# DeltaNet's last chunk of 16 tokens: four heads stacked on the partitions

## The chip, the cores and the metric

One core of a Trainium2 chip runs the whole program in one launch. The metric is the device time of that launch in microseconds, lower is better. TensorE (PE) does the matmuls, VectorE (DVE) and ScalarE (ACT) the elementwise work, GpSimd (POOL) some masks, and SyncE (SP) issues the DMAs. TensorE's clock has two levels, 1.2 and 2.4 GHz; the profile shows it as a granted clock of 0.50 and 1.00.

## The reference

A decoder trunk on 256 tokens and 16 meta tokens ahead of them (272 in all, model width 2048): one gated DeltaNet layer with its MLP, then one differential-attention layer with its MLP, everything in float32. The DeltaNet layer has 32 value heads of width 128; two value heads share a query and key head. Per head it is, cut to what matters:

```python
proj = h @ w_in                                   # q, k, v, gate, b, a
qkv = silu(causal_depthwise_conv(qkv, conv_w))
q, k = l2_normalize(q) * 128 ** -0.5, l2_normalize(k)
beta = sigmoid(b_logit); g = -exp(a_log) * softplus(a_logit + dt_bias)
# by chunks, with the state S (128 x 128):
G = cumsum(g); decay = exp(G_i - G_j) below the diagonal
a_kk = strictly_lower((k * beta) @ k.T * decay)
u, w = solve(I + a_kk, [v * beta, k * beta * exp(G)])
v_new = u - w @ S
o = (q * exp(G)) @ S + ((q @ k.T) * decay) @ v_new
S = S * exp(G_last) + (k * exp(G_last - G)).T @ v_new
o = rms_norm(o, o_norm) * silu(z);  out = o @ w_out
```

## The kernel before

`trunk` keeps the activations on chip with features on the partitions and tokens in the free dimension, 128x272 tiles. Each float32 weight product is three matmuls (`mm3`, L146): the weight and the activation are each split into a high and a low part, and hi x hi (L152), lo x hi (L155) and hi x lo (L156) are added in PSUM. A weight tile of 1 MB is loaded by SP (L120, into `wraw`, three buffers), then halved: ACT makes `whi` of 128x1024 (L137), DVE `wlo` (L139), in a ring of three. One half serves 8 steps of 3 matmuls. These matmuls, 272 columns each, are called the big products below.

The DeltaNet layer (`gdn`, L503) works on 8 groups of 4 value heads. For each group the big products of `w_in` run (`ps_in`, later `ps_out` for `w_out`), and between them the small work of the delta rule. The tokens are cut into chunks of 128, 128 and 16 (`CH`), numbered 0, 1 and 2; chunk 2 of 16 tokens is the one that the change is about. Per group and chunk:

- `keys` and `stats` (L636): transposes of q and k by chunk (`ps_kn`, L649), and sums of squares on ACT (`sqk`, L654).
- `products` (L666): the norms, a broadcast load of the group's cumulated log decays (`gb`, L686), masks on POOL (L688, L690), k by k and k by q (`ps_u`, L706), decays on ACT (`dec`, L710), and their product on DVE (`UA`, L712). The 16x16 diagonal blocks go to DRAM (L718, L721).
- `solve` (L737): inverts the 16x16 blocks of the group's heads, and loads the inverses (`DT`, L755; `DT3` for chunk 2, L757).
- `values` (L759): transposes of v (`ps_v`, L771) and scaled copies (`nv`, L773).
- `core` (L796): the recurrence. Per chunk, `ps_ks` (L880) and `R` (L884), for the long chunks the merging of the block inverses (`ps_e`, L840, is its first matmul), then `ps_w` (L916), `w` (L924), the state (`ps_s`, L929), `ps_o` (L941), `ov` (L947), squares (L951), the norm (L959 to L963, with `rsqrt` at L105 to L111), the scale (L966), and in `turned` the transposes back (`ps_ot`, L810) and their eviction into `oT` (L812). `oT` is split into `oh` and `ol` (L979, L980), on which the big products of `w_out` wait.

In chunk 2 every one of these is done per head, on 16 partitions: four `ps_w` of 16x16 weights, four `ps_o`, four `R`, and so on; `ps_ks` puts k and q of a key head side by side in `KQ3` (48 columns of weights).

The order of the work is written by `Flow` (L57): generators with due times stand in a heap, and each step of `mm3` moves its clock by `flow.tick(3 * N / 2400.0)`; what is due is emitted there. A scheduler then sets the order of each engine's queue. Group 7, the last, uses the shorter steps of `STEP7`, and its chunk 2 stands directly ahead of the last big products of `w_out`. In `decays` (L542), once at the head, the log decays of all heads are cumulated and stored to DRAM (`g_dram`, L584), from which every group's `gb` is read. SP also issues the loads of small constants between the first weight loads.

Of the kernel before, what the change touches and what calls it, by code (L numbers as in the profile page):

```python
# [31 lines left out]
GB = 4  # L32
HOLD = 1
# [469 lines left out]
def gdn(ctx, tc, a, e):  # L503
# [21 lines left out]
    gt = ctx.enter_context(tc.tile_pool(name="gt", bufs=2))  # L525
    gk = ctx.enter_context(tc.tile_pool(name="gk", bufs=4))
# [15 lines left out]
    def decays(ps):  # L542
# [29 lines left out]
        nc.vector.reciprocal(bt, bt)  # L572
        yield GATES[1]
# [10 lines left out]
        nc.sync.dma_start(g_dram, rows)  # L584
        G, GL = gnat[:, 0], gnat[:, 1]
# [5 lines left out]
        nc.scalar.activation(eLast, eLast, AF.Exp)  # L591
        gated.append(True)

    g_dram = dram.tile([32, L], F32, name="g_dram", bufs=1)
# [9 lines left out]
    DT3 = gc.tile([NM, HB, NM], F32, name="DT3")  # L604
    KQ3 = gc.tile([P, 2, 64], F32, name="KQ3")
# [30 lines left out]
    def keys(b):  # L636

        g = {"done": False, "free": False, "laid": False, "gates": 0, "values": 0, "chunk": 0,
             "prev": gs[-1] if gs else None}
        st = gt.tile([P, 2, 3, 2], F32, tag="st", name="st")  # L640
        nc.vector.memset(st, 1.0)
        kq = g["kq"] = gk.tile([P, 2, 2, L], F32, tag="kq", name="kq", bufs=2)
        kn = g["kn"] = gk.tile([P, 2, 2, P], F32, tag="kn", name="kn", bufs=2)

        def stats(h, t):
            yield SLACKST
            pk = psk.tile([P, 512], F32, tag="k", name="ps_kn")
            for c, (o, n) in enumerate(CH):
                nc.tensor.transpose(pk[:n, c * P:(c + 1) * P], kq[:, h, t, o:o + n], ident)  # L649
            if t == 0:  # L650
                nc.scalar.copy(kn[:, :, h, :], pk[:, :256].rearrange("p (c d) -> p c d", d=P))
            for c, (o, n) in enumerate(CH):
                sq = gt.tile([P, P], F32, tag="dec", name="sqk", bufs=2)
                nc.scalar.activation(sq[:n], pk[:n, c * P:(c + 1) * P], AF.Square, accum_out=st[:n, t, c, h:h + 1])  # L654
            if (h, t) == (1, 0):
                yield from products(b, g, st)

        for h in range(2):
            for t, m in ((1, 2 * b + h), (0, 16 + 2 * b + h)):
                ps = proj(m)  # L660
                conv_silu(ps, m, kq[:, h, t, :])
                flow.add(stats(h, t))
        return g

    def products(b, g, st):
        kq, prev = g["kq"], g["prev"]  # L666
# [15 lines left out]
        nc.vector.tensor_tensor(sup, sup, heads(eLast, b), ALU.mult)
        nc.vector.tensor_scalar(rq, rs[:, 1, :, :, None].broadcast_to([P, 3, 2, 2]), P ** -0.5, None, ALU.mult)
# [6 lines left out]
        nc.gpsimd.affine_select(gb[:NM, :, 256:L], gb[:NM, :, 256:L], pattern=[[0, HB], [1, NM]], base=0,  # L690
                                channel_multiplier=-1, compare_op=ALU.is_ge, fill=NEG)
# [3 lines left out]
        for c, (o, n) in enumerate(CH):  # L695
            while prev and prev["chunk"] < min(c, 1):
                yield 1.0
            if c < 2:
                ua = gk.tile([P, HB, 2, P], F32, tag="UA", name="UA", bufs=3)
            else:  # L700
                ua = gk.tile([NM, HB, 2, NM], F32, tag="UA3", name="UA3", bufs=2)
            UA.append(ua)
            for h in range(2):
# [3 lines left out]
                for r in range(2):  # L707
# [4 lines left out]
                    nc.vector.scalar_tensor_tensor(ua[:, hv], pu_v, negc[:n, c, h, r:r + 1],  # L712
                                                   dec[:n, None, :n].broadcast_to([n, 2, n]), ALU.mult, ALU.mult)
                yield UGAP
            if c < 2:
                for bl in range(8):
                    q = slice(NM * bl, NM * bl + NM)
                    nc.sync.dma_start(scr[c, :, bl].rearrange("h j i -> j h i"), ua[q, :, 0, q])  # L718
                below(ua, NM)
            else:  # L720
                nc.sync.dma_start(scr3.rearrange("h j i -> j h i"), ua[:, :, 0, :])  # L721
# [15 lines left out]
    def solve(scr, scr3):  # L737
# [19 lines left out]
        nc.sync.dma_start(DT3, scr4.rearrange("h m j -> m h j"))  # L757

    def values(b, g):  # L759
# [3 lines left out]
        def turned(hv, vt):  # L763
# [3 lines left out]
            if not nv:  # L767
                nv.extend(gk.tile([P, HB, P], F32, tag="nv", name="nv", bufs=4) for _ in CH)
            pv = psk.tile([P, 512], F32, tag="k", name="ps_v")
            for c, (o, n) in enumerate(CH):  # L770
                nc.tensor.transpose(pv[:n, c * P:(c + 1) * P], vt[:, o:o + n], ident)  # L771
            for c, (o, n) in enumerate(CH):
                nc.scalar.activation(nv[c][:n, hv], pv[:n, c * P:(c + 1) * P], AF.Copy,  # L773
                                     scale=g["nk"][:n, c, hv // 2:hv // 2 + 1])
            g["values"] += 1

        for hv in range(HB):
# [4 lines left out]
            conv_silu(ps, m, vt)  # L782
            flow.add(turned(hv, vt))
# [11 lines left out]
    def core(b, g):  # L795
# [7 lines left out]
        def turned(c, o, n, ov):  # L803
# [5 lines left out]
            for hv in range(HB):  # L809
                nc.tensor.transpose(pT[:, hv * n:(hv + 1) * n], ov[:n, hv], ident[:n, :n])  # L810
# [9 lines left out]
        ms = gt.tile([P, len(CH), HB], F32, tag="o_ms", name="o_ms")  # L820
# [42 lines left out]
        for c, (o, n) in enumerate(CH):  # L863
            if c == 0:
                R = nv[0]
            else:
                left = lambda h, t: kq[:, h, t, o:o + n]
                pS, pSv = bank("ps_ks")
                if c < 2:
                    pQ, pQv = bank("ps_qs")  # L870
                    banks = ((pS[:n], 0), (pQ[:n], 1))
                else:
# [3 lines left out]
                    banks = ((pS[:32 + n], 0),)  # L876
                    pQv = pSv[32:]
                for ps, t in banks:
                    for h in range(2):
                        nc.tensor.matmul(ps[:, 256 * h:256 * h + 256], left(h, t), S[:, 2 * h:2 * h + 2, :],  # L880
                                         start=True, stop=True)
                R = work("R")
                for hv in range(HB):
                    nc.vector.scalar_tensor_tensor(R[:n, hv], pSv[:n, hv], neG[:n, c, HB * b + hv:HB * b + hv + 1],  # L884
                                                   nv[c][:n, hv], ALU.mult, ALU.add)
                ov = work("ov")
                nc.scalar.copy(ov[:n], pQv[:n])
# [23 lines left out]
            else:  # L911
                z, dt = R, DT3
            yield step
            _, pw = bank("ps_w")
            for hv in range(HB):
                nc.tensor.matmul(pw[:n, hv], dt[:, hv, :], z[:n, hv], start=True, stop=True)  # L916
            if c == 2:
                g["free"] = True
            if c < 2:
# [3 lines left out]
            w = work("w")  # L923
            nc.scalar.copy(w[:n], pw[:n])  # L924
            yield step
            if c < 2:
# [12 lines left out]
            _, po = bank("ps_o")  # L939
            for hv in range(HB):  # L940
                nc.tensor.matmul(po[:n, hv], UA[c][:, hv, 1, :], w[:n, hv], start=True, stop=True)  # L941
            if c == 0:
                ov = work("ov")
                nc.scalar.activation(ov, po, AF.Copy, scale=-1.0)
            else:
                for hv in range(HB):
                    nc.vector.scalar_tensor_tensor(ov[:n, hv], ov[:n, hv], eG[:n, c, HB * b + hv:HB * b + hv + 1],  # L947
                                                   po[:n, hv], ALU.mult, ALU.subtract)

            for hv in range(HB):  # L950
                nc.scalar.activation(po[:n, hv], ov[:n, hv], AF.Square, accum_out=ms[:n, c, hv:hv + 1])  # L951
            outs.append((c, o, n, ov))
            if b == NB - 1 or c == len(CH) - 1:
                c0 = outs[0][0]
                k = HB * len(outs)
                pn = n if len(outs) == 1 else P
                mc = ms[:pn, c0:c + 1].rearrange("p c h -> p (c h)")
                rqc = rq[:pn, c0:c + 1].rearrange("p c h r -> p (c h r)")
# [3 lines left out]
                ri = rsqrt(mc, "rso%d" % k, [P, k], pn)  # L962
                nc.vector.tensor_tensor(ri, ri, rqc, ALU.mult)  # L963
                for i, (cc, oo, nn, ot) in enumerate(outs):
                    for hv in range(HB):
                        nc.scalar.activation(ot[:nn, hv], ot[:nn, hv], AF.Copy, scale=ri[:nn, HB * i + hv:HB * i + hv + 1])  # L966
# [311 lines left out]
```

## Time and profile before

| | |
|---|---|
| three runs | 3022.2, 3023.15, 3023.69 us (median 3023.15) |
| profiled execution | 3024.88 us, span 3023.1 us, mean granted clock 0.993 |
| TensorE busy | 2981.0 us, 99% of the span, 23747 matmuls |
| DVE, ACT, POOL busy | 1943.6 us (64%), 1490.1 us (49%), 205.2 us (7%) |
| DMA | 488.36 MB, 92468 packets, 29104 of them under 512 B |

A busy time alone says little here, because matmuls overlap: a row's duration runs from the start of a matmul to its end in the pipeline, and the next starts before that. So the starts of neighbouring rows are what is compared. In the rows of the timeline, `128*16` stands for the weights' partitions and columns, then comes the moving operand; `x4` says that the row holds several instructions; a float32 matmul that is not split counts as two, so four products stand as `x8`. Times in square brackets are idle time before, with what ended it.

### The profile page before, as it was taken

The page shows a single profiled execution, that of the slowest core. Times are in us where ns is not written, and L with a number is a line of the kernel's source. Part 1 is how long each engine was busy: PE and PEld are TensorE (multiplying, and loading weights), DVE is VectorE, ACT ScalarE, POOL GpSimd, SP SyncE. Part 2 cuts the span into 40 slices and gives each one's busy share as a digit, 9 for nine tenths or more (in the row PEclk, how much of TensorE's full clock was granted, in tenths as well). Part 3 has the DMA queues.
Part 4 walks back from the last instruction along what each step waited for, and adds up shares of the span by engine and source line. Part 5 has one row for each costly group of instructions (what it writes and reads, how often), then busy time and mean ns, then how long its engine had stood idle before and what let it go on. Part 6 is the DMA issues. An engine that isn't in the chain of part 4 may idle for free. (4 is left out here: it accounts for less than half of the span.)

```text
span 3023.1 us, 57162 instructions
## 1 busy us (share of the span) xinstructions
PE 2981.0 (99%) x23747; PEld 2924.3 (97%) x23747; DVE 1943.6 (64%) x3452; ACT 1490.1 (49%) x2735; POOL 205.2 (7%) x208
## 2 busy tenths in 40 slices
PE   8999999999999899999999999999999999999998
PEld 8999999999999799999999999999999999999998
DVE  7777576776867674555555558777757555555555
ACT  4565555465555454444344434455555444444443
POOL 0100010000100220000000004300004000000001
PEclk9999999999999899999999999999999999999999
DMA  5433343434434444454544443433354555555553
GB/s 211 151 137 122 142 151 135 156 124 153 146 120 144 153 155 180 168 180 169 179 170 176 173 176 145 153 140 138 143 194 165 184 187 190 183 193 183 191 187 112
DMA packets 92468, 488.36 MB, mean 162 GB/s; under 512 B 29104, under 2 KB 32528, under 8 KB 34736
## 3 DMA queue, kind: packets, MB, share of 16 engines
q1 hardware_dynamic: 92208, 484.70, 44.6%
q8 instruction: 187, 3.06, 0.4%
q14 instruction: 73, 0.60, 0.1%
HBM read 481.41 MB, written 3.25 MB: 160 GB/s over the span
## 5 line engine op out<-in xcount | busy, mean ns | idle before, releaser
L139 DVE TENSOR_TENSOR wlo<-wraw,whi 128x1024 fp32r<-128x1024 f32 x872 | 1070.0, 1229 | 770.8 <-ACT whi L137 769.5
L137 ACT ACTIVATE whi<-wraw 128x1024 fp32r<-128x1024 f32 x890 | 940.2, 1059 | 1145.7 <-PE ps_dn L156 432.1
L152 PE MATMUL ps_dn<-yh,whi 128*128 128x272 f32 (+1 forms) x2048 | 583.2, 285 | 0.0
L152 PE MATMUL ps_up<-xh,whi 128*128 128x272 f32 (+1 forms) x2048 | 582.8, 285 | 0.0
L156 PE MATMUL ps_dn<-yl,whi 128*128 128x272 f32 (+1 forms) x2048 | 582.3, 284 | 0.0
L155 PE MATMUL ps_up<-xh,wlo 128*128 128x272 f32 (+1 forms) x2048 | 581.0, 285 | 0.2 <-DVE wlo L139 0.2
L155 PE MATMUL ps_dn<-yh,wlo 128*128 128x272 f32 (+1 forms) x2048 | 580.9, 284 | 0.0
L156 PE MATMUL ps_up<-xl,whi 128*128 128x272 f32 (+1 forms) x2048 | 580.3, 285 | 0.1
L152 PE MATMUL ps_in<-xh,whi 128*128 128x272 f32 x1520 | 460.2, 303 | 0.0
L156 PE MATMUL ps_in<-xl,whi 128*128 128x272 f32 x1520 | 441.6, 291 | 0.8 <-DVE xl L320 0.8
L155 PE MATMUL ps_in<-xh,wlo 128*128 128x272 f32 x1520 | 441.3, 291 | 0.0
L152 PEld LDWEIGHTS ps_up<-xh,whi 128*128 128x128 f32 x2048 | 385.9, 188 | 0.5 <-ACT xh L401 0.4
L155 PEld LDWEIGHTS ps_dn<-yh,wlo 128*128 128x128 f32 x2048 | 386.0, 188 | 0.0
L152 PEld LDWEIGHTS ps_dn<-yh,whi 128*128 128x128 f32 x2048 | 385.5, 188 | 0.0
L156 PEld LDWEIGHTS ps_up<-xl,whi 128*128 128x128 f32 x2048 | 384.8, 188 | 0.5 <-DVE xl L409 0.5
L155 PEld LDWEIGHTS ps_up<-xh,wlo 128*128 128x128 f32 x2048 | 384.6, 188 | 0.5 <-DVE wlo L139 0.5
L156 PEld LDWEIGHTS ps_dn<-yl,whi 128*128 128x128 f32 x2048 | 384.8, 188 | 0.0
L152 PEld LDWEIGHTS ps_in<-xh,whi 128*128 128x128 f32 x1520 | 287.2, 189 | 7.7 <-issue 4.9
L155 PEld LDWEIGHTS ps_in<-xh,wlo 128*128 128x128 f32 x1520 | 287.6, 189 | 1.6 <-issue 0.4
L156 PEld LDWEIGHTS ps_in<-xl,whi 128*128 128x128 f32 x1520 | 286.6, 189 | 1.4 <-DVE xl L320 1.0
L475 DVE TENSOR_TENSOR acc<-acc,ps_dn 128x272 f32<-128x272 f32 (+1 forms) x224 | 95.9, 428 | 122.1 <-PE ps_dn L156 121.4
L152 PE MATMUL ps_at<-xh,whi 128*128 128x272 f32 x512 | 154.5, 302 | 0.0
(313 smaller groups left out, 4476.9 us busy)
## 6 DMA issues: line engine op xcount, KB each, us to landing
wraw<-w_up SPq DMA_DIRECT2D x128, 1024.0 KB, 4.8
wraw<-w_down SPq DMA_DIRECT2D x128, 1024.0 KB, 4.8
wraw<-w_in SPq DMA_DIRECT2D x97, 1024.0 KB, 4.8
wraw<-w_out SPq DMA_DIRECT2D x32, 1024.0 KB, 4.9
wraw<-w_kv SPq DMA_DIRECT2D x32, 1024.0 KB, 4.8
wraw<-w_q SPq DMA_DIRECT2D x16, 1024.0 KB, 5.8
wraw<-w_o SPq DMA_DIRECT2D x16, 1024.0 KB, 5.6
gb<-g_dram SPq DMA_DIRECT2D x8, 544.0 KB, 5.6
```

Of the source, the lines that this page charges most:

```text
L137: nc.scalar.activation(hi, part, AF.Copy)
L139: inst = eng.tensor_tensor(lo, part, hi.bitcast(F32), ALU.subtract)
L152: one = nc.tensor.matmul(ps, wh, rh, start=(k == 0), stop=False)
L155: nc.tensor.matmul(ps, wl, rh, start=False, stop=False)
L156: ring["mm"] = nc.tensor.matmul(ps, wh, rl, start=False, stop=(k == nk - 1))
L475: nc.vector.tensor_tensor(acc[:, m, :N], acc[:, m, :N], ps[:, :N], ALU.add)
```

## The change

Chunk 2 of a group is computed for its four heads at once, stacked on 64 partitions (`TQ` = 4 x 16), with block-diagonal tiles: the masked decays are zero outside the diagonal blocks, and `DT3` becomes a 64x64 tile of zeros with four 16x16 blocks. Per group:

- `kn`: the four 16-token transposes go; a new tile `kc` (128x128, each head's k and q of the last 16 tokens, two ACT copies) is transposed once, with one square on ACT instead of four.
- `ps_u`: one product of 64x128 instead of two of 16x32; one `dec`, one `UA`. The store `scr3` and the load `DT3` are four DMAs each instead of one.
- `ps_v`: a new tile `vc` gathers the last 16 tokens of the four heads (four ACT copies) and is transposed once instead of four times; one `nv`.
- `ps_ks`: `KQ3` is laid out so that four products with 128x128 weights, each zero but for its own head's columns, add up in one 128x128 result: k of the four heads on partitions 0 to 63, q on 64 to 127. It replaces two products with 48 columns of weights and 256 moving columns.
- `R`, `ps_w`, `w`, `ps_o`, `ov`, square, scale, `ps_ot`: one each instead of four (`w` was one).
- One more mask on POOL, a column for the norms of chunk 2 (`ms`, `rq`, `negc`).
- Once, in `decays`: betas and log decays of the last 16 tokens are loaded in the stacked layout (`beta3`, 4 loads; `G3`, 8 loads of 16x8 single elements), and `eG3`, `neG3` are made from them.

Cut to its core:

```diff
@@ decays @@
+        nc.sync.dma_start(b_dram, bt[:NM, 2, :])
...
         nc.sync.dma_start(g_dram, rows)
+        by_head = lambda t: t.rearrange("i (b h) -> h i b", h=HB)
+        for h in range(HB):
+            nc.sync.dma_start(beta3[NM * h:NM * h + NM], by_head(b_dram)[h])
+            for t in range(2):
+                q = TQ * t + NM * h
+                nc.sync.dma_start(G3[q:q + NM], g_dram[:, 256:L].rearrange("(b h) i -> h i b", h=HB)[h])
...
+        nc.scalar.activation(eG3, G3, AF.Exp)
+        nc.vector.tensor_scalar(neG3, eG3, -1.0, None, ALU.mult)
+        nc.vector.tensor_scalar(G3, G3, -1.0, None, ALU.mult)
@@ keys, stats @@
-            for c, (o, n) in enumerate(CH):
+            for c, (o, n) in enumerate(LATE):
                 nc.tensor.transpose(pk[:n, c * P:(c + 1) * P], kq[:, h, t, o:o + n], ident)
@@ products @@
+        kc = gk.tile([P, 2, HB, NM], F32, tag="kc", name="kc", bufs=1)
+        for t in range(2):
+            nc.scalar.copy(kc[:, t].rearrange("p (h r) i -> p h r i", r=2),
+                           kq[:, :, t, 256:L][:, :, None, :].broadcast_to([P, 2, 2, NM]))
...
+        nc.tensor.transpose(pk[:, :P], kc, ident)
...
-            else:
-                ua = gk.tile([NM, HB, 2, NM], F32, tag="UA3", name="UA3", bufs=2)
+            if c == 2:
+                ua = gk.tile([TQ, 2, TQ], F32, tag="UA3", name="UA3", bufs=2)
...
+                nc.tensor.matmul(pu[:TQ, :P], kc[:, :TQ], kc, start=True, stop=True)
...
+                nc.scalar.activation(dec.rearrange("p (h i) -> p h i", i=NM), gb3, AF.Exp, bias=G3[:TQ, b:b + 1])
+                nc.vector.scalar_tensor_tensor(ua, pu[:TQ, :P].rearrange("p (t i) -> p t i", t=2), negc[:TQ, 8:9],
+                                               dec[:, None, :].broadcast_to([TQ, 2, TQ]), ALU.mult, ALU.mult)
+                yield UGAP
+                for h in range(HB):
+                    q = slice(NM * h, NM * h + NM)
+                    nc.sync.dma_start(scr3[h], ua[q, 0, q])
+                break
...
-                nc.sync.dma_start(scr3.rearrange("h j i -> j h i"), ua[:, :, 0, :])
@@ solve @@
-        nc.sync.dma_start(DT3, scr4.rearrange("h m j -> m h j"))
+        for h in range(HB):
+            q = slice(NM * h, NM * h + NM)
+            nc.sync.dma_start(DT3[q, q], scr4[h])
@@ values @@
+            if hv == HB - 1:
+                nc.tensor.transpose(pv[:TQ, 256:384], g["vc"].rearrange("p h i -> p (h i)"), ident)
+                nc.scalar.activation(nv[2], pv[:TQ, 256:384], AF.Copy, scale=g["nk"][:TQ, 4:5])
@@ core @@
+            if c == 2:
+                nc.tensor.transpose(pT[:, :TQ], ov[TQ:, 0, :], ident[TQ:, TQ:])
+            else:
+                for hv in range(HB):
+                    nc.tensor.transpose(pT[:, hv * n:(hv + 1) * n], ov[:n, hv], ident[:n, :n])
...
-                    nc.scalar.copy(KQ3.rearrange("p h (t i) -> p h t i", i=32)[:, :, :, 0:n], kq[:, :, :, o:o + n])
-                    left = lambda h, t: KQ3[:, h, 0:32 + n]
...
+                nc.scalar.copy(KQ3[:, :, TQ - NM:].rearrange("p h (t x) -> p h t x", t=2)[:, :, :, 0:n], kq[:, :, :, o:o + n])
+                pS, _ = bank("ps_ks")
+                for hv in range(HB):
+                    w0 = TQ - NM - NM * hv
+                    nc.tensor.matmul(pS[:, :P], KQ3[:, hv // 2, w0:w0 + P], S[:, hv, :], start=(hv == 0), stop=(hv == HB - 1))
...
+                nc.vector.scalar_tensor_tensor(R[:TQ, 0], pS[:TQ, :P], neG3[:TQ, b:b + 1], nv[2], ALU.mult, ALU.add)
...
+                nc.tensor.matmul(pw[:TQ, :P], DT3, R[:TQ, 0], start=True, stop=True)
...
+                nc.scalar.copy(w[:TQ, 0], pw[:TQ, :P])
...
+                nc.tensor.matmul(po[:, :P], UA[2].rearrange("p t i -> p (t i)"), w[:TQ, 0], start=True, stop=True)
+                nc.vector.scalar_tensor_tensor(ov[TQ:, 0], ov[TQ:, 0], eG3[TQ:, b:b + 1], po[TQ:, :P],
+                                               ALU.mult, ALU.subtract)
+                nc.scalar.activation(po[TQ:, :P], ov[TQ:, 0], AF.Square, accum_out=ms[TQ:, 8:9])
```

How the order of the queues moves is shown at two places. TensorE, the last chunk of group 7, ahead of the last big products (`L152`, `ps_out`). Before:

```order
L880 MATMUL ps_ks<-S,KQ_262 48x256 x2
L916 MATMUL ps_w<-R,DT_261 16x128 x4
L810 MATMUL ps_ot<-ident,ov 128x128
L941 MATMUL ps_o<-w,UA_10889 16x128
L810 MATMUL ps_ot<-ident,ov 128x128
L941 MATMUL ps_o<-w,UA_10889 16x128
L810 MATMUL ps_ot<-ident,ov 128x128
L941 MATMUL ps_o<-w,UA_10889 16x128
L810 MATMUL ps_ot<-ident,ov 128x128
L941 MATMUL ps_o<-w,UA_10889 16x128
L810 MATMUL ps_ot<-ident,ov 128x16 x4
L152 MATMUL ps_out<-oh,whi 128x272
```

With the change (`ps_ot` of 128x128 belongs to chunk 1, all else to chunk 2):

```order
L939 MATMUL ps_ks<-S,KQ_268 128x128 x4
L947 MATMUL ps_w<-R_12051,DT_266 64x128
L864 MATMUL ps_ot<-ident,ov 128x128
L953 MATMUL ps_o<-w_12057,UA_10762 128x128
L864 MATMUL ps_ot<-ident,ov 128x128 x3
L861 MATMUL ps_ot<-ident,ov_12053 128x64
L153 MATMUL ps_out<-oh,whi 128x272
```

One `ps_o` stands behind the first transpose of chunk 1, where four alternated with the four transposes.

SP, the head of the program, from the store of the log decays to the first store of group 0's diagonal blocks and, with the change, to the loads for its solve. Before:

```order
L584 DMA g_dram<-g_rows 32x272
L686 DMA gb<-g_dram 128x1088
L120 DMA wraw<-w_in 128x2048 x2
L718 DMA scr<-UA 16x4x16 x16
L721 DMA scr_696<-UA_820 16x4x16
L120 DMA wraw<-w_in 128x2048
L745 DMA na<-scr 64x256
```

With the change (`G_254` is `G3`, `scr_731` is `scr3`):

```order
L587 DMA g_dram<-g_rows 32x272
L121 DMA wraw<-w_in 128x2048
L593 DMA G_254<-g_dram 16x8x1 x8
L717 DMA gb<-g_dram 128x1088
L121 DMA wraw<-w_in 128x2048 x2
L762 DMA scr<-UA 16x4x16 x8
L121 DMA wraw<-w_in 128x2048
L762 DMA scr<-UA 16x4x16 x8
L744 DMA scr_731<-UA_854 16x16 x4
L787 DMA na<-scr 64x256
```

The eight loads of `G3` and one weight load stand between the store of the log decays and group 0's `gb`.

## Rows read from the trace of the kernel before

**Rows 1.** Busy by stretch: length; PE, PEld, DVE, ACT, POOL; PE clock, DMA, GB/s.
```profile
750.00:900.00 150.00, 150.00 (x1174) 145.65 (x1173) 109.33 (x238) 85.06 (x205) 11.46 (x14) 1.00 0.40 137
1003.00:1020.00 17.00, 7.74 (x31) 3.07 (x29) 8.13 (x36) 8.24 (x29) 0.00 (x0) 0.60 0.12 48
1020.00:1023.50 3.50, 3.41 (x15) 3.41 (x16) 1.76 (x5) 1.00 (x4) 0.00 (x0) 0.50 0.28 52
```

**Rows 2.** Costliest groups: busy, mean ns, idle before them and what ended it.
```profile
L155 PE MATMUL ps_up<-xh,wlo 128*128 128x272 f32 (+1 forms) x2048 | 581.0, 285 | 0.2 <-DVE wlo L139 0.2
```

**Rows 3.** Timeline of PE (start, duration, instruction): four full 128x128 products between big ones.
```profile
131.07 0.29 PE L156 MATMUL ps_in<-xl,whi 128*128 128x272 f32 x1
131.20 0.29 PE L152 MATMUL ps_in<-xh,whi 128*128 128x272 f32 x1
131.32 1.05 PE L840 MATMUL ps_e<-e,us 128*128 128x128 f32 x8
132.13 0.37 PE L155 MATMUL ps_in<-xh,wlo 128*128 128x272 f32 x1
132.34 0.29 PE L156 MATMUL ps_in<-xl,whi 128*128 128x272 f32 x1
```

**Rows 4.** Timeline of PE: chunk 2's four ps_w, 16x16 weights.
```profile
407.82 0.29 PE L156 MATMUL ps_in<-xl,whi 128*128 128x272 f32 x1
408.04 1.04 PE L916 MATMUL ps_w<-R,DT 16*16 16x128 f32 x8
409.02 0.40 PE L152 MATMUL ps_in<-xh,whi 128*128 128x272 f32 x1
```

**Rows 5.** Timeline of PE: chunk 2's two ps_ks.
```profile
403.82 1.06 PE L880 MATMUL ps_ks<-S,KQ 128*48 128x256 f32 x4
404.82 0.39 PE L152 MATMUL ps_in<-xh,whi 128*128 128x272 f32 x1
```

**Rows 6.** Timeline of PE: the three ps_v transposes of a head.
```profile
400.76 0.49 PE L771 MATMUL ps_v<-ident,vt 128*128 128x128 f32 x3
401.01 0.37 PE L152 MATMUL ps_in<-xh,whi 128*128 128x272 f32 x1
```

**Rows 7.** Timeline of PE: chunk 2's four ps_ot transposes together.
```profile
310.63 0.41 PE L810 MATMUL ps_ot<-ident,ov 16*128 16x16 f32 x4
310.98 0.39 PE L152 MATMUL ps_in<-xh,whi 128*128 128x272 f32 x1
```

**Rows 8.** Timeline of PE: one ps_ot transpose of chunk 2 alone.
```profile
214.90 0.23 PE L810 MATMUL ps_ot<-ident,ov 16*128 16x16 f32 x1
215.06 0.39 PE L155 MATMUL ps_in<-xh,wlo 128*128 128x272 f32 x1
```

**Rows 9.** Timeline of PE, DVE and ACT: the tail of group 7.
```profile
1008.80 0.47 PE L810 MATMUL ps_ot<-ident,ov 128*128 128x128 f32 x1 [1.27 <-ACT ov L966]
...
1012.02 0.60 PE L941 MATMUL ps_o<-w,UA 16*16 16x128 f32 x2
1012.13 0.75 DVE L812 SCALAR_TENSOR_TENSOR oT<-ps_ot,gain_h,oT 128x512 f32<-128x512 f32 x1 [3.82 <-PE ps_ot L810]
...
1015.72 0.15 DVE L959 TENSOR_TENSOR o_ms<-o_ms,sc_rq 16x4 f32<-16x4 f32 x1 [1.83 <-ACT ps_o L951]
...
1017.65 1.28 ACT L966 ACTIVATE ov<-ov,rs_y 16x128 f32<-16x128 f32 x4 [1.96 <-DVE rs_y L963]
...
1018.11 1.16 PE L810 MATMUL ps_ot<-ident,ov 16*128 16x16 f32 x4 [5.48 <-ACT ov L966]
...
1020.09 0.60 PE L152 MATMUL ps_out<-oh,whi 128*128 128x272 f32 x1 [0.83 <-ACT oh L979]
```

**Rows 10.** Page's DMA issues (KB, us to landing), then the timeline of ACT and SP.
```profile
onorm<-onorm SPq DMA_DIRECT2D x1, 0.5 KB, 10.1
...
77.97 0.68 ACT L710 ACTIVATE dec<-gb,ngG 128x128 f32<-128x128 f32 x2
...
123.02 3.92 SPq L755 DMA_DIRECT2D DT<-scr  x8
```

More of the change, by code (lines that the diff above doesn't have):

```diff
@@ L32 @@
 GB = 4
+TQ = HB * NM
 HOLD = 1
@@ L603, in gdn @@
     nc.vector.memset(DT, 0.0)
-    DT3 = gc.tile([NM, HB, NM], F32, name="DT3")
-    KQ3 = gc.tile([P, 2, 64], F32, name="KQ3")
+    DT3 = gc.tile([TQ, TQ], F32, name="DT3")
+    nc.vector.memset(DT3, 0.0)
+    KQ3 = gc.tile([P, 2, 2 * TQ + TQ - NM], F32, name="KQ3")
     nc.vector.memset(KQ3, 0.0)
@@ L711, in products @@
                                          bias=ngG[:n, c, HB * b + hv:HB * b + hv + 1])
-                    nc.vector.scalar_tensor_tensor(ua[:, hv], pu_v, negc[:n, c, h, r:r + 1],
+                    nc.vector.scalar_tensor_tensor(ua[:, hv], pu_v, negc[:n, 4 * c + hv:4 * c + hv + 1],
                                                    dec[:n, None, :n].broadcast_to([n, 2, n]), ALU.mult, ALU.mult)
                 yield UGAP
[L715 to L720, printed above, removed]
-                nc.sync.dma_start(scr3.rearrange("h j i -> j h i"), ua[:, :, 0, :])
+            for bl in range(8):
+                q = slice(NM * bl, NM * bl + NM)
+                nc.sync.dma_start(scr[c, :, bl].rearrange("h j i -> j h i"), ua[q, :, 0, q])
+            below(ua, NM)
         g["laid"] = True
@@ L782, in values @@
             conv_silu(ps, m, vt)
+            if hv == 0:
+                g["vc"] = gt.tile([P, HB, NM], F32, tag="vc", name="vc", bufs=2)
+            nc.scalar.copy(g["vc"][:, hv], vt[:, 256:L])
             flow.add(turned(hv, vt))
@@ L910, in core @@
                 nc.vector.tensor_tensor(z, z, p3, ALU.add)
[L911 to L919, printed above, removed]
+                yield step
+                _, pw = bank("ps_w")
+                for hv in range(HB):
+                    nc.tensor.matmul(pw[:n, hv], dt[:, hv, :], z[:n, hv], start=True, stop=True)
                 ws = work("ws")
@@ L922, in core @@
                     nc.scalar.activation(ws[:, hv], pw[:, hv], AF.Copy, scale=sup[:, c, hv // 2, hv % 2:hv % 2 + 1])
[L923 to L926, printed above, removed]
+                w = work("w")
+                nc.scalar.copy(w[:n], pw[:n])
+                yield step
                 pS2, pS2v = bank("ps_s2")
@@ L938, in core @@
                 S = S2
[L939 to L945, printed above, removed]
-                for hv in range(HB):
[L947 to L951, printed above, removed]
+                _, po = bank("ps_o")
+                for hv in range(HB):
+                    nc.tensor.matmul(po[:n, hv], UA[c][:, hv, 1, :], w[:n, hv], start=True, stop=True)
+                if c == 0:
+                    ov = work("ov")
+                    nc.scalar.activation(ov, po, AF.Copy, scale=-1.0)
+                else:
+                    for hv in range(HB):
+                        nc.vector.scalar_tensor_tensor(ov[:n, hv], ov[:n, hv], eG[:n, c, HB * b + hv:HB * b + hv + 1],
+                                                       po[:n, hv], ALU.mult, ALU.subtract)
+                for hv in range(HB):
+                    nc.scalar.activation(po[:n, hv], ov[:n, hv], AF.Square, accum_out=ms[:n, HB * c + hv:HB * c + hv + 1])
             outs.append((c, o, n, ov))
             if b == NB - 1 or c == len(CH) - 1:
[L954 to L958, printed above, removed]
+                cols = slice(HB * outs[0][0], min(9, HB * (c + 1)))
+                mc, rqc = ms[:, cols], rq[:, cols]
+                k = cols.stop - cols.start
                 nc.vector.tensor_tensor(mc, mc, rqc, ALU.mult)
@@ L961, in core @@
                 nc.vector.tensor_scalar(mc, mc, 1.0 / P, EPS, ALU.mult, ALU.add)
-                ri = rsqrt(mc, "rso%d" % k, [P, k], pn)
+                ri = rsqrt(mc, "rso%d" % k, [P, k])
                 nc.vector.tensor_tensor(ri, ri, rqc, ALU.mult)
                 for i, (cc, oo, nn, ot) in enumerate(outs):
-                    for hv in range(HB):
-                        nc.scalar.activation(ot[:nn, hv], ot[:nn, hv], AF.Copy, scale=ri[:nn, HB * i + hv:HB * i + hv + 1])
+                    if cc == 2:
+                        nc.scalar.activation(ot[TQ:, 0], ot[TQ:, 0], AF.Copy, scale=ri[TQ:, k - 1:k])
+                    else:
+                        for hv in range(HB):
+                            nc.scalar.activation(ot[:, hv], ot[:, hv], AF.Copy, scale=ri[:, HB * i + hv:HB * i + hv + 1])
                     flow.add(turned(cc, oo, nn, ot), STEP7[1] if b == NB - 1 else OTURN + TGAP * i)
```

105 lines of the change are left out of this document (63 added, 42 removed).

## The prediction

> **What bounds the kernel now.** I read the busy times by stretch first. In a stretch of the DeltaNet layer TensorE is busy 150.00 of 150.00 us at full granted clock, with DVE at 109.33 and ACT at 85.06 [rows 1]: the matmul queue is the time there, and each product taken out of it comes off the end, if nothing else steps in. Next the waits: the matmul that waits longest for converted weights does so for 0.2 us in the whole run [rows 2], so the conversions of ACT and DVE keep ahead. Only one place is different. In group 7's last chunk TensorE is busy 7.74 of 17.00 us and at a low clock [rows 1]: there a chain of small steps sets the time, and the rows of that chain are read one by one [rows 9].
>
> So the change is priced twice: as TensorE time for groups 0 to 6 and the early part of group 7, and as a chain for the tail of group 7. After the DeltaNet layer nothing changes.
>
> **The price of a small product between big ones.** Matmuls overlap, so their own durations mislead. What counts is how late the next big product starts. Big ones follow each other at 0.13 us (131.07 to 131.20 in [rows 3]). Four full 128x128 products with 128 columns in between: from the big product ahead to the one behind 131.20 to 132.13, 0.93, and 0.21 on to the next, less two ordinary steps (0.26): 0.88, which is 0.20 each and 0.08 for the interruption [rows 3]. The same with 16 rows (ps_w of chunk 2): 1.20 + 0.22 - 0.26 = 1.16 [rows 4]. There the first starts 0.22 behind the big product instead of 0.12, and the four cost 0.28 more than full ones: I call this the gap. The other small groups are worked out in the same way from the start of the small product and of the big one behind it, with 0.22 ahead and about 0.22 behind as in [rows 3, 4]: ps_ks with 48 columns of weights 0.22 + 1.00 + 0.22 - 0.26 = 1.18 for two products [rows 5]; four ps_ot transposes of 16 rows 0.22 + 0.35 + 0.22 - 0.26 = 0.53 [rows 7]; one of them alone 0.22 + 0.16 + 0.22 - 0.26 = 0.34 [rows 8]. Three ps_v transposes, the 16-token one among them, start without delay, 0.13 ahead and 0.21 behind as the full ones: 0.13 + 0.25 + 0.21 - 0.26 = 0.33, so 0.11 each and no gap [rows 6].
>
> **TensorE, per group.** kn: four transposes of 16 tokens go, -0.44; the new one of kc, +0.11. ps_v: four become one, -0.33. ps_u: two single products at 0.34 (taken as a single small one, [rows 8]) become one of 64x128, which I price with the gap, 0.20 + 0.08 + 0.28 = 0.56: -0.12. ps_ks: 1.18 becomes four full products that accumulate, 0.88: -0.30. ps_w and ps_o: each 1.16 becomes one 64-row product, 0.56: -0.60 each. ps_ot: 0.53 becomes 0.34, -0.19. Sum -2.47; for groups 0 to 6, -17.3. In groups 0 and 6 the four ps_ot stood apart, at 4 x 0.34 instead of 0.53: another -0.83 each, -1.7. Group 7 before its tail (kn, kc, ps_v, ps_u): -0.8.
> No row shows a 64-row product. From below, it pays no gap: three per group, 3 x 0.28 x 7 = 5.9 less. From above, the transposes of kc and vc also pay as a small group of their own, 0.34 instead of 0.11: 2 x 0.23 x 8 = 3.7 more. I keep the gap, because the one form in between, ps_ks with 48 columns of weights, shows it too: 1.18 against 0.88 for the same columns at full size [rows 3, 5].
>
> **The tail of group 7.** Before, the last chunk's four ps_o alternated with the four transposes of chunk 1, 1008.80 to 1012.62; then DVE did ps_ot's eviction (0.75) and four ov, ACT four squares, DVE a norm from 1015.72 to 1017.65, ACT the scale, TensorE four ps_ot to 1019.27, and TensorE restarted at 1020.09 [rows 9]. Now one ps_o stands behind the first transpose. With that transpose at 1008.8 as before (its ACT work has a copy more in front, its norm four R fewer between: taken as even), ps_o ends at 1009.8 and the three other transposes, 0.4 each, at 1011.0; ov and the one square are done beside them. The eviction ends at 1011.8, the norm (1.93) at 1013.8, the first of the scales, now the only one, releases ps_ot 0.46 later (1017.65 to 1018.11), at 1014.25; one ps_ot instead of four ends at 1014.7; the same 0.82 on (1019.27 to 1020.09), the restart is at 1015.5. That is -4.6, of which I take **-4.5**. If chunk 1's scale comes 1.5 us later it is -3; if also the small products there run 1.5 us quicker than at the half clock, -6. The clock stays at half (0.50) for 3.5 us behind the restart [rows 1]: the level comes back at its own time, and half of 3.5, 1.7 us, is the bound on both sides.
>
> **ACT, DVE, POOL.** Per group dec, squares, scales, nv, R, ov and UA lose three instructions of four each; six small copies, one more mask on POOL and two tiny DVE operations come. Beside a TensorE that is never waiting in these stretches this is worth nothing; if that cover went, DVE still has 40 us free in 150 [rows 1].
>
> **SP's queue.** Each group has six more DMA issues (the scr3 store and the DT3 load, one to four each), 6 x 0.49 = 2.9 us by the eight that took 3.92 [rows 10]. Weight loads stand behind them. The queue already issued such runs of nine with waits on converted weights of 0.2 us in all [rows 2], so runs of twelve are priced at 0; from above, 2.9 us per group if there were no cover.
>
> **The head.** Once, eight loads of G3 go ahead of group 0's gb on SP: 8 x 0.49 = 3.9 us of issue [rows 10], so gb comes that much later, and later still if these loads, whose pieces are 4 bytes, are slow. What waits for G3 and gb are ACT's dec and DVE's operations on G3 and UA, with weight conversions queued behind both. But in the new order ACT reaches the first dec after 20 halves of weights instead of 17: 3 x 24 big products x 0.13 = 9 us behind the 77.97 of before [rows 10], at 87. So 9 - 3.9 = 5 us are free before ACT stands, and two converted halves, 6 us, before TensorE does: 11 us of cover. I take +0.5, between 0 and 6.
> A rule speaks against these loads. The row nearest to them is onorm, 128 pieces of 4 bytes: 10.1 us to land, though of only 0.5 KB [rows 10]. The Trainium skill, "DMA: Bandwidth & Descriptors", Rules for kernel authors, says that a strided last dimension lowers to one descriptor per element and should be rearranged to be contiguous; onorm's 10.1 us agrees. By the forecast the loads overlap and the head costs 0.5; by that row, one behind the other, it costs 66, the last rival below.
>
> **Sum.** -17.3 - 1.7 - 0.8 - 4.5 + 0.5 = -23.8. The profiled execution took 3024.88: 3001.1. The median of the runs lies 1.7 lower, so **2999.4 us**.
>
> **Rivals.**
> 1. The head costs more: the G3 loads take 16 to 30 us beyond their issue. ACT and DVE stand at dec and at G3, and TensorE for what exceeds the 11 us of cover, 5 to 19: 3004 to 3018. For it: weight loads of 1 MB stand on the same queue ahead of them, and the row of onorm. Against it: the DT loads below.
> 2. No gap with 64 rows: 2993.5. Nothing in the trace shows a quicker form of less than 128 rows.
> 3. Nothing is won: the freed TensorE time is given back in waits for weights, 3023. The 0.2 us of waiting and DVE's 109 of 150 speak against it [rows 1, 2].
> 4. Slower: the eight G3 loads go one after the other at onorm's 10.1 us, 81 us in all, and ACT and DVE stand behind them. TensorE stands for 81 - 3.9 - 11 = 66: 3065. It decides for slower from 45 us on (24 to make good, 6 more, 11 of cover, 3.9 of issue), 5.6 us per load. For it: the 10.1 of the only load of this kind [rows 10]. Against it: onorm ran among the first 1 MB loads of the program, and eight DT loads of 64-byte pieces were issued within 3.92 us and all used by TensorE 4.4 us after the last (126.94 to 131.32) [rows 3, 10], so loads of one queue do overlap.
>
> **Chances and range.** Forecast 0.74 (its own range 2991 to 3007: gap -5.9 and tail -1.5 below, new transposes, head and tail above), rival 1 0.12, rival 2 0.04, rival 3 0.05, rival 4 0.05. 0.2% is 6 us, about what a measurement of this kernel can tell from no change. Faster by more: 0.74 + 0.12 + 0.04 = 0.90; same 0.05; slower 0.05. The range 2990 to 3011 takes in the forecast and the nearer half of rival 1.
>
> **What would show it.** ps_w and ps_o of chunk 2 as one product each, the big product behind it 0.8 us or so after the one in front; ps_ks with no late start. TensorE's restart in the tail at 1015.5 less the 19 us that came off before it, near 996. No wait above 1 us in front of products with weights around 80 to 150 us, and ACT's first dec at its place without a wait for gb. Wrong would be: a stop of TensorE there, 64-row products that cost as much as four, or new waits for wlo.

## The result and the profile after

The changed kernel takes 3007.28 us (median of four runs, 3007.16 to 3007.38) against 3023.42 for the kernel before: a ratio of 0.9947 with a 95% interval of 0.993 to 0.9964. It is faster, by 16.1 us where 24.0 were forecast; the time lies in the stated range. The profiled execution took 3007.38 us with a span of 3004.7.

The DeltaNet layer did what was said of it. The timeline of TensorE after the change, group 0, chunk 2: the four `ps_ks`, the one `ps_w`, the one `ps_o`.

```profile
189.90 0.29 PE L157 MATMUL ps_in<-xl,whi 128*128 128x272 f32 x1
190.03 1.05 PE L939 MATMUL ps_ks<-S,KQ 128*128 128x128 f32 x8
190.84 0.38 PE L153 MATMUL ps_in<-xh,whi 128*128 128x272 f32 x1
191.05 0.29 PE L156 MATMUL ps_in<-xh,wlo 128*128 128x272 f32 x1
...
194.21 0.29 PE L157 MATMUL ps_in<-xl,whi 128*128 128x272 f32 x1
194.43 0.43 PE L947 MATMUL ps_w<-R,DT 64*64 64x128 f32 x2
194.79 0.40 PE L153 MATMUL ps_in<-xh,whi 128*128 128x272 f32 x1
195.03 0.29 PE L156 MATMUL ps_in<-xh,wlo 128*128 128x272 f32 x1
...
198.40 0.29 PE L157 MATMUL ps_in<-xl,whi 128*128 128x272 f32 x1
198.62 0.48 PE L953 MATMUL ps_o<-w,UA 64*128 64x128 f32 x2
199.03 0.39 PE L153 MATMUL ps_in<-xh,whi 128*128 128x272 f32 x1
199.26 0.29 PE L156 MATMUL ps_in<-xh,wlo 128*128 128x272 f32 x1
```

Read as in [rows 3, 4]: `ps_ks` 0.94 + 0.21 - 0.26 = 0.89, without the late start; `ps_w` 0.58 + 0.24 - 0.26 = 0.56, where the four took 1.16; `ps_o` 0.63 + 0.23 - 0.26 = 0.60. The 64-row products start 0.22 behind the big one, so the gap is still paid.

The tail of group 7, where [rows 9] answer:

```profile
983.32 1.05 PE L939 MATMUL ps_ks<-S,KQ 128*128 128x128 f32 x8
...
989.11 0.48 PE L864 MATMUL ps_ot<-ident,ov 128*128 128x128 f32 x1 [3.48 <-ACT ov L1030]
989.51 0.79 PE L953 MATMUL ps_o<-w,UA 64*128 64x128 f32 x2
990.24 0.90 PE L864 MATMUL ps_ot<-ident,ov 128*128 128x128 f32 x3
...
991.17 0.75 DVE L866 SCALAR_TENSOR_TENSOR oT<-ps_ot,gain_h,oT 128x512 f32<-128x512 f32 x1 [0.48 <-PE ps_ot L864]
991.84 0.15 DVE L1020 TENSOR_TENSOR o_ms<-o_ms,sc_rq 128x1 f32<-128x1 f32 x1
...
993.89 0.40 ACT L1027 ACTIVATE ov<-ov,rs_y 64x128 f32<-64x128 f32 x1 [2.67 <-DVE rs_y L1024]
994.34 0.36 PE L861 MATMUL ps_ot<-ident,ov 64*128 64x64 f32 x1 [3.20 <-ACT ov L1027]
...
995.53 0.60 PE L153 MATMUL ps_out<-oh,whi 128*128 128x272 f32 x1 [0.82 <-ACT oh L1043]
```

TensorE restarts at 995.53, 24.56 before the 1020.09 of [rows 9]; the forecast was 996. In the kernel before, the same chain starts with

```profile
1003.24 1.06 PE L880 MATMUL ps_ks<-S,KQ 128*48 128x256 f32 x4
```

The head, in the same timeline, POOL, ACT and SP:

```profile
73.92 0.34 SPq L587 DMA_DIRECT2D g_dram<-g_rows  x1
...
75.43 4.13 SPq L593 DMA_DIRECT2D G<-g_dram  x8
79.61 0.78 SPq L717 DMA_DIRECT2D gb<-g_dram  x1
...
83.69 1.10 POOL L719 TENSOR_SCALAR_AFFINE_SELECT gb<-gb 128x1024 f32<-128x1024 f32 x1 [45.14 <-DMA gb<-g_dram]
...
87.22 0.68 ACT L755 ACTIVATE dec<-gb,ngG 128x128 f32<-128x128 f32 x2
```

Before:

```profile
70.55 0.34 SPq L584 DMA_DIRECT2D g_dram<-g_rows  x1
72.06 0.34 SPq L686 DMA_DIRECT2D gb<-g_dram  x1
...
76.03 1.10 POOL L688 TENSOR_SCALAR_AFFINE_SELECT gb<-gb 128x1024 f32<-128x1024 f32 x1 [38.16 <-DMA gb<-g_dram]
```

The eight loads take 4.13 us to issue. POOL's mask starts when `gb` lands, at 83.69, and ACT reaches the first `dec` at 87.22 (87 was forecast), with no wait in its row. TensorE doesn't stop in this stretch of the changed kernel (windows view, columns as in [rows 1]):

```profile
30.00:137.00 107.00, 107.00 (x835) 104.66 (x833) 87.60 (x184) 59.42 (x134) 9.51 (x12) 1.00 0.51 182
```

So 24.6 us are won at the end of the DeltaNet layer, and only 18.4 are left in the span. What is lost lies where the change has no instruction. The windows view, the same two stretches of the two MLPs. Before:

```profile
1300.00:1700.00 400.00, 400.00 (x3173) 400.00 (x3173) 215.74 (x263) 164.01 (x199) 0.00 (x0) 1.00 0.49 175
2400.00:2800.00 400.00, 400.00 (x3411) 400.00 (x3411) 226.44 (x274) 176.49 (x221) 0.00 (x0) 1.00 0.52 187
```

After, with the tail of group 7 and its restart ahead of them:

```profile
983.00:995.50 12.50, 4.19 (x21) 2.73 (x20) 7.08 (x30) 5.55 (x20) 0.00 (x0) 0.68 0.17 71
995.50:1001.20 5.70, 5.67 (x25) 5.67 (x26) 1.94 (x5) 1.36 (x4) 0.00 (x0) 0.50 0.01 3
...
1300.00:1700.00 400.00, 400.00 (x3174) 400.00 (x3173) 216.43 (x264) 164.49 (x200) 0.00 (x0) 1.00 0.49 175
2400.00:2800.00 400.00, 400.00 (x3383) 400.00 (x3382) 227.84 (x282) 175.60 (x217) 0.00 (x0) 1.00 0.52 185
```

TensorE is busy all the time at the full granted clock in both. In the first MLP (272 columns) it does as many matmuls as before. In the second (256 columns, without the meta tokens) it does 3383 in 400 us instead of 3411: a step of 400 / 3383 = 118.24 ns instead of 117.27. Followed by the start of the same big product in the two traces, the lead is 23.6 us in the first MLP (1.0 is lost on the clock behind the tail), 25.2 at 2189 us, in the attention's output products, where the columns have become 256; from there it falls by 0.8 to 1.1 us with every 1000 products, through the whole second MLP, and is 18.6 at the last one. The last one before, after, and in e1, an experiment below:

```profile
3006.90 0.28 PE L156 MATMUL ps_dn<-yl,whi 128*128 128x256 f32 x1
...
2988.32 0.28 PE L157 MATMUL ps_dn<-yl,whi 128*128 128x256 f32 x1
...
2983.13 0.28 PE L158 MATMUL ps_dn<-yl,whi 128*128 128x256 f32 x1
```

The 1.6 us by which the lead grows between the two MLPs go with the clock, at two places around the start of the attention. Before and after:

```profile
1835.90:1842.80 6.90, 6.33 (x29) 6.06 (x30) 2.50 (x11) 0.00 (x0) 0.21 (x1) 0.51 0.40 152
1897.40:1904.20 6.80, 6.80 (x34) 6.74 (x35) 3.42 (x12) 1.70 (x4) 0.00 (x0) 0.50 0.31 131
...
1813.60:1817.00 3.40, 3.40 (x17) 3.23 (x16) 1.03 (x7) 0.00 (x0) 0.00 (x0) 0.50 0.72 292
1875.10:1878.50 3.40, 3.40 (x18) 3.40 (x18) 2.10 (x10) 1.32 (x2) 0.00 (x0) 0.51 0.01 5
```

It stays at half for 3.4 us instead of 6.8 or 6.9. In e1 it is 6.8 at both places, as before, and its lead over the kernel before does not grow there (23.85 us ahead of them, 23.75 behind).

### The profile page after: what moved, and what is told of

Read it like the earlier page. It is cut to its first block, busy times and chain, and to the rows that moved or that the text cites. A ratio compares the mean times of both kernels' runs of the same rounds, so it can differ in the third digit from the quotient of the medians.

```text
span 3004.7 us, 56783 instructions
## 1 busy us (share of the span) xinstructions
PE 2965.7 (99%) x23595; PEld 2920.7 (97%) x23595; DVE 1929.2 (64%) x3391; ACT 1465.2 (49%) x2616; POOL 214.3 (7%) x216
## 2 busy tenths in 40 slices
DMA packets 94992, 488.32 MB, mean 163 GB/s; under 512 B 31632, under 2 KB 35056, under 8 KB 37264
```

## The experiments

What could slow an unchanged loop? The small buffers of the change: group 7's chunk 2 is now normed alone, with one column, and `rsqrt` makes new buffers `rso1` for it, 192 bytes per partition. They push `yh`, `yl` (the MLP's activations) and the second of the two rings of weight halves that take turns in the MLP by 192 bytes, and with them buffers that no big product reads, such as `hT` (the residual) and the MLP's row scratch. In bytes modulo 512, by the addresses that the allocator gives, the first ring and `xh`, `xl` stand at 96 in both kernels; `yh`, `yl` and the second ring at 416 before and at 96 after.

**e1 and e2: the addresses, there and back.** Theory A says that the addresses do it, theory B the place in TensorE's instruction stream (23595 matmuls instead of 23747). e1 lets the new norm use the buffers of `rso4`; no instruction changes:

```diff
-        y = npool.tile(shape, F32, tag=tag + "_y", name="rs_y")[:n]
+        k = x.shape[1]
+        y = npool.tile(shape, F32, tag=tag + "_y", name="rs_y")[:n, :k]
...
-                ri = rsqrt(mc, "rso%d" % k, [P, k])
+                ri = rsqrt(mc, "rso%d" % max(k, HB), [P, max(k, HB)])
```

> The changed kernel, with one thing altered: the norm of group 7's last chunk takes a buffer that exists already, so that no new small buffers (192 bytes per partition) are allocated, and the activations yh, yl and the second ring of weight halves stand at the addresses that they had in the kernel before. No instruction is added or removed. Theory A (in the second MLP and the attention projections, with 256 columns, the step from one big product to the next depends on where weights and activations stand in SBUF): the step there returns from 118.3 to about 117.4 ns, and the time to about 3007.3 - 6.5 = 3001. Theory B (it depends on the number of PE instructions ahead, that is on the phase at which the stream arrives): step and time stay, 118.3 ns and 3007.

Measured: 3000.91 us, ratio 0.9925 (0.991 to 0.9939). The windows view of e1:

```profile
2400.00:2800.00 400.00, 400.00 (x3410) 400.00 (x3410) 229.50 (x283) 177.53 (x220) 0.00 (x0) 1.00 0.52 187
```

3410 matmuls: the old step is back, and the last big product starts 23.77 us before that of the kernel before. Theory B falls: TensorE's instructions are those of the changed kernel. e2 puts the same 192 bytes into the kernel before:

```diff
                 ri = rsqrt(mc, "rso%d" % k, [P, k], pn)
+                if b == NB - 1 and c == len(CH) - 1:
+                    nc.gpsimd.memset(npool.tile([P, 24], F32, tag="pad", name="pad"), 0.0)
```

> The kernel before, with an unused buffer of 192 bytes per partition at the place where the change brings its new ones, so that yh, yl and the second weight ring stand where the changed kernel has them; everything else as before. Theory A: the DeltaNet layer takes its old time, the step of the big products with 256 columns goes from 117.4 to 118.3 ns, and the time from 3023.4 to about 3030. Theory B: nothing changes, 3023.4 within 0.5.

Measured: 3030.88 us, ratio 1.0021 (1.0012 to 1.003), and in its windows view:

```profile
2400.00:2800.00 400.00, 400.00 (x3383) 400.00 (x3382) 224.76 (x272) 174.88 (x218) 0.00 (x0) 1.00 0.51 185
```

An unused buffer costs the kernel before 6.7 us against the 3024.18 that it took in the same session. Theory A is shown from both sides.

**e4 to e8: what about the addresses.** Unused buffers in up to three places, on top of e1; the table gives the offsets, modulo 512, that come of their sizes. The first of the three in e4:

```diff
+    pads = ctx.enter_context(tc.tile_pool(name="pad1", bufs=1))
+    nc.gpsimd.memset(pads.tile([P, 80], F32, name="pad1"), 0.0)
     xpool = ctx.enter_context(tc.tile_pool(name="xpool", bufs=1))
```

> The kernel of e1 with three unused buffers (320, 192 and 192 bytes per partition) placed so that in every big product the activations stand at 416 and the weights at 96 modulo 512 bytes; in the changed kernel both stand at 96, in e1 half of the products have them apart. Theory A, with the relative offset as what counts: every product is of the quicker kind, the step with 256 columns falls below e1's 117.4 ns to 115 to 116.5, and the time is 5 to 15 us under e1's. If the offsets of each tile alone count, or only the ring's halves: the step is as e1's or slower. Theory B: no difference from the changed kernel.

> The kernel of e1 with 192 unused bytes ahead of the second weight ring alone: both weight rings stand at 96 modulo 512, xh and xl at 96, yh and yl stay at 416. After e4 theory A is divided. A1: what counts is that the two weight rings, which take turns every 24 products, stand at different offsets, so that the phase between weights and activations jumps at each turn. Then all steps with 256 columns are 118.3 ns, as in the changed kernel, and the time is 3007.5. A2: the offset between weights and activations counts; then the products on yh and yl (half of the MLP) keep the quick steps of e1 and the time is near 3004.

> The kernel of e1 with yh and yl moved to 96 modulo 512, where xh and xl stand, and the second weight ring held at 416 (the first is at 96). A1 (the rings' difference): the steps stay as quick as in e1, 117.4 ns on average, 3001. A2: steps of a new mean in the half on yh and yl, time between 3001 and 3007. If the activations' place alone had mattered: 118.3 ns there, 3004 or more.

> The kernel of e1 with the second weight ring at 224 modulo 512 (128 from the first, instead of 320 from it, which is 64 modulo 256); yh and yl as in e1. A1: there is a jump at each turn of the rings, so steps below 118.3 ns, a mean between 115 and 118, and a time of 2992 to 3006; which of them A1 alone doesn't say. If only the difference of e1 were quick: 118.3 ns, 3007.5.

> The kernel of e1 with all weights at 96 and all activations at 128 modulo 512. The activations of one step of 3 products lie 1088 bytes behind those of the step before, 64 modulo 256, so the shifts of e4 (a multiple of 64) only renumber the steps; a shift of 32 is a new offset. A1: no jump at the turns, so one locked pattern: if the grid of 64 counts alone, 118.3 ns and 3007.5; if the offset within 64 counts too, another constant mean, anywhere from 113 to 119 ns. The pattern must repeat every 12 products in either case.

Measured, with matmuls in 2400 to 2800 us (second MLP) and 1300 to 1700 us (first MLP) from the windows view:

| kernel | ring 1, ring 2 | xh xl, yh yl | second MLP | first MLP | time, ratio (95%) |
|---|---|---|---|---|---|
| changed | 96, 96 | 96, 96 | 3383 | 3174 | 3007.28, 0.9947 (0.993 to 0.9964) |
| e1 | 96, 416 | 96, 416 | 3410 | 3172 | 3000.91, 0.9925 (0.991 to 0.9939) |
| e4 | 96, 96 | 416, 416 | 3383 | 3174 | 3007.93, 0.9949 (0.9934 to 0.9963) |
| e5 | 96, 96 | 96, 416 | 3383 | 3174 | 3008.66, 0.995 (0.9935 to 0.9965) |
| e6 | 96, 416 | 96, 96 | 3402 | 3170 | 3002.48, 0.9931 (0.9916 to 0.9946) |
| e7 | 96, 224 | 96, 416 | 3402 | 3178 | 3001.6, 0.9927 (0.9911 to 0.9944) |
| e8 | 96, 96 | 128, 128 | 3367 | 3195 | 3003.54, 0.9933 (0.9918 to 0.9948) |

e4 missed: having activations and weights apart in every product gains nothing, 3383 as in the changed kernel. e5 settles between A1 and A2: with the rings alike, `yh` and `yl` where e1 has them, the count is 3383 again. A row of e5:

```profile
2400.00:2800.00 400.00, 400.00 (x3383) 400.00 (x3382) 228.35 (x281) 175.54 (x219) 0.00 (x0) 1.00 0.52 185
```

Whenever the two rings differ (e1, e6, e7) it is 3402 to 3410. In the traces with the rings alike the steps of the second MLP repeat every 12 products to within 1 ns (most often 119, 118, 120, 119, 117, 118, 119, 117, 118, 118, 115, 122); with rings that differ, the steps change at each turn of the rings, and stretches of 12 lie between 114.4 and 119.7 on average. In e8 all activations stand 32 bytes off all weights: 3367 in the second MLP is slower, 3195 in the first, where the rings move the count by 4 at most, quicker. Its rows:

```profile
1300.00:1700.00 400.00, 400.00 (x3195) 400.00 (x3194) 217.64 (x265) 165.43 (x202) 0.00 (x0) 1.00 0.49 177
2400.00:2800.00 400.00, 400.00 (x3367) 400.00 (x3367) 227.36 (x281) 175.36 (x217) 0.00 (x0) 1.00 0.52 185
```

That it matters whether the rings are alike is shown. No run moves the first ring, so the second ring's own place could be the cause instead; but the starts in the traces speak against it. The `ps_dn` products of the second MLP that read the first ring have weights at 96 and activations at 416 in e1 as in e5, and their step is 116.5 ns on average in e1 and 118.3 in e5. So it depends on where the other ring stands. What the weight and activation reads do to each other inside, so that a step is 115 or 122 ns, no run shows.

**e3: the gap of small tiles.** On e1, chunk 2's products with zeros up to 128 rows and columns, in short:

```diff
-                nc.tensor.matmul(pu[:TQ, :P], kc[:, :TQ], kc, start=True, stop=True)
+                nc.tensor.matmul(pu[:, :P], kc, kc, start=True, stop=True)
...
-                nc.tensor.matmul(pw[:TQ, :P], DT3, R[:TQ, 0], start=True, stop=True)
+                nc.tensor.matmul(pw[:, :P], DT3, R[:, 0], start=True, stop=True)
...
-                nc.tensor.transpose(pT[:, :TQ], ov[TQ:, 0, :], ident[TQ:, TQ:])
+                nc.tensor.transpose(pT[:, :P], ov[:, 0, :], ident)
+                pT = pT[:, TQ:]
```

> The kernel of e1 with the last chunk's products ps_u, ps_w, ps_o and the transpose ps_ot brought to full 128x128 weights (zero rows and columns where the four heads have none). Theory C (a product with weights of fewer than 128 rows or columns between full ones pays a gap of 0.26 to 0.31 us, whatever it computes): per group -0.26 (ps_u), -0.26 (ps_w), -0.31 (ps_o), -0.2 (ps_ot), about 1.0, over 7 groups -7, so 2994 if theory A holds and e1 is at 3001. Rival (the time of these islands is that of one product in a chain, not of its form): within 1 us of e1.

Measured: 2992.96 us, ratio 0.9901 (0.9885 to 0.9918), the expected 7 below e1 and one more. In the two traces 7.6 us of it are there at the first MLP, and 2.4 come in the attention, where the clock is at half for 3.4 and 3.5 us in this execution and for 6.8 and 6.8 in that of e1. Its `ps_w` in the timeline of TensorE:

```profile
193.71 0.29 PE L158 MATMUL ps_in<-xl,whi 128*128 128x272 f32 x1
193.84 0.38 PE L951 MATMUL ps_w<-R,DT 128*128 128x128 f32 x2
193.97 0.38 PE L154 MATMUL ps_in<-xh,whi 128*128 128x272 f32 x1
194.19 0.29 PE L157 MATMUL ps_in<-xh,wlo 128*128 128x272 f32 x1
```

0.26 + 0.22 - 0.26 = 0.22 instead of 0.56: four times the array for the same numbers, and a third of a microsecond less. The Trainium skill, "TensorEngine Tiling (Array Packing)", Key Properties, says that a change of the tiling mode drains TensorE; this pair of rows agrees, with 0.34 us for a product of 64x64 weights between full ones, though no row shows the drain itself.

Not every small form pays it. In the changed kernel the transpose of `vc` has weights of 128 rows and 64 columns and stands behind two full ones:

```profile
408.29 0.29 PE L157 MATMUL ps_in<-xl,whi 128*128 128x272 f32 x1
408.42 0.38 PE L816 MATMUL ps_v<-ident,vt 128*128 128x128 f32 x2
408.63 0.27 PE L818 MATMUL ps_v<-ident,vc 128*64 128x128 f32 x1
408.66 0.37 PE L153 MATMUL ps_in<-xh,whi 128*128 128x272 f32 x1
408.87 0.29 PE L156 MATMUL ps_in<-xh,wlo 128*128 128x272 f32 x1
```

0.37 + 0.21 - 0.26 = 0.32 for the three, 0.11 each as in [rows 6]. `ps_u` has weights of the same 128x64 but is no transpose, and it does pay (0.55 in the changed kernel, 0.21 in e3).

**e9 and e10: both together.** e3 with 32 bytes ahead of `xh` (e9), and with the second ring placed apart again (e10).

> The kernel of e3 (full tiles) with one unused buffer of 32 bytes per partition ahead of xh: xh, xl at 128, yh, yl and the second weight ring at 448, the first ring at 96 modulo 512. In e8 activations 32 bytes off made the 272-column steps of the first MLP 0.8 ns quicker and the 256-column ones slower. If the two effects add up (first MLP quicker by 5 us, rings apart in the second): 2986 to 2992. If the 32 bytes cost in the second MLP what they bring in the first: e3's 2993 within 2.

> As e9, with the second weight ring at 416 modulo 512 (32 bytes off yh and yl too, 64 modulo 256 from the first ring, as in e3). A1 says a jump at each turn of the rings, so steps with 256 columns under e8's 118.9 ns; with the first MLP 5 us quicker 2984 to 2992. If activations 32 bytes off take away what the jump brings: 2996 or more.

Measured: e9 2992.19, ratio 0.9897 (0.9883 to 0.9912); e10 2991.91, ratio 0.9892 (0.9876 to 0.9909). The first MLP is quicker (3186 and 3197 matmuls in 400 us), the second slower (3388 and 3381 against e3's 3410), and in time the three can't be told apart. In e9 only the products on the first ring stand 32 bytes off (modulo 64), and in its first MLP the `ps_dn` step changes at each turn: 125.1 ns on the first ring, 126.0 on the second. This shows in one trace that the 32 bytes between weights and activations matter in themselves. In the second MLP the rings' difference brings less with activations 32 bytes off: 3381 in e10 against e8's 3367, where it brought 27 without (3410 against 3383).

## Why the prediction was right and where it failed

A row of the kernel before, windows view, that the first point needs:

```profile
122.50:125.90 3.40, 3.40 (x17) 3.40 (x16) 1.78 (x3) 1.50 (x6) 2.46 (x4) 0.50 0.10 15
```

- **The price of the small products**: right for the single ones: `ps_ks` 0.89 (0.88 said), `ps_w` 0.56 (0.56), `ps_o` 0.60 (0.56). In sum 17.3 + 1.7 + 0.8 = 19.8 us were to go before the tail, and four big products before the tail the same product starts 19.83 us earlier in the changed kernel. That the two meet so closely is luck, for the 19.83 hold more than the small products. In the row above, behind a wait of 1.86 us for `kq` that ended at 121.29, the clock is at half and the big products follow each other at 0.226 us instead of 0.126. This costs 1.5 us that the changed kernel doesn't lose. TensorE also waits 0.7 us less in the changed kernel between 66 us and the tail, and stands 0.7 us behind at 27 us, ahead of the first small products. So some 18.3 us are left for the products (an estimate from these numbers), 1.5 less than the sum.
- **The gap with 64 rows** (kept, against rival 2): right, and e3 shows that it hangs on the form of the tile. It is 0.34 for `ps_w` by its own pair of rows, 0.28 by the reading before.
- **The tail**: right. From `ps_ks` to the restart 12.21 us instead of 16.85, as 1003.24 to 1020.09 in the trace before; -4.64 where -4.6 was worked out and -4.5 taken. Of the clock a bound of 1.7 was given: it stays at 0.50 for 5.7 us behind the restart instead of 3.5; half of the difference is 1.1 us, and the lead falls by 1.0 there.
- **The head**: right at 0 instead of +0.5. Rivals 1 and 4 fall: `gb` lands 7.7 us later than the 76 of before, ahead of ACT's place. Of these, 3.4 are there already at the store of the log decays (73.92 instead of 70.55), and 4.1 are the issue of the eight loads. The loads overlap; one after the other at onorm's 10.1 us [rows 10] would have put `gb` past 150. The rule that the prediction takes from the Trainium skill, "DMA: Bandwidth & Descriptors", Rules for kernel authors, is about the number of pieces: one descriptor per element. The trace agrees: packets under 512 B go from 29104 to 31632, and the eight loads have 1024 elements. Here that number shows in no wait of TensorE, and hardly in the issue: 4.13 us, where eight loads of 64-byte pieces took 3.92 [rows 10].
- **Rival 3**: falls. The longest wait for `wlo` is still 0.2 us.
- **What failed** is the sentence that after the DeltaNet layer nothing changes. No instruction does, but 192 bytes of new buffers made the two weight rings alike, and from the attention's output products to the end of the second MLP the kernel took 6.6 us longer. That is the larger part of the 7.9 between the forecast and the time. With the addresses of before (e1) the last product comes 23.77 us earlier, where the sum had -23.8; this closeness too is partly luck, since e1 lost 0.8 on the clock behind the tail and its small products brought some 1.5 less than said, while the kernel before lost 1.5 at 122.5. The time is 3000.91 where 2999.4 was said. The 1.5 that stay are within what its runs (3000.3 to 3001.45) and those of the kernel before in the same session (3022.79 to 3026.55) differ by.

## What to carry to other kernels

A product with weights of fewer than 128 rows or columns between full ones paid some 0.3 us for its form here, and so did a transpose of fewer than 128 rows; a transpose of 128 rows and 16 or 64 columns did not. So stack first, and then fill up with zeros to the full array. Where a loop that a change doesn't touch gets a per cent slower, count its matmuls in a fixed stretch of both traces and compare the addresses of its operands before looking for a cause in the change: here buffers of 192 bytes were worth 6.4 us in the changed kernel (e1) and 6.7 in the one before (e2). A forecast for such a change should hold some microseconds in its range for where the buffers come to lie.

## What the runs showed of the hardware

With TensorE always busy at the full granted clock, the step of 256-column products depends on where their operands lie in SBUF: 117.3 to 117.6 ns with two weight rings at different offsets modulo 512, 118.2 with equal ones (3410 to 3402, and 3383 in 400 us), 118.8 with equal rings and activations 32 bytes off (3367). The 272-column products hardly react to the rings (3170 to 3178), but to the 32 bytes they do: 125.2 ns instead of 126.0 (3195 and 3174). Nothing else in the windows differs that would explain it: granted clock and DMA share are the same, and the busy times of ACT and DVE within 3%.

Between big products, `ps_w` with weights of 64x64 cost 0.56 us and, filled up with zeros to 128x128, 0.22; a transpose with weights of 128x64 cost 0.11, as a full one does. Of eight loads of 128 single elements each, issued in 4.13 us, none held up TensorE.
